# Splitting whole weight tiles of four k-tiles at once, with two raw buffers and three buffers each for hi and lo

## The chip, the cores and the metric

The kernel runs on one core of a Trainium2 chip. The metric is the device time of one launch in microseconds (us), less is better. The engines are called as in the profile: PE (TensorE matmuls; PEld is its weight load), DVE (VectorE), ACT (ScalarE), POOL (GpSimd) and SP (SyncE, which here only issues DMAs). Each engine takes its instructions strictly in the order of its own queue.

## What is computed

One inference step of one layer of a hybrid decoder, for a prompt group (256 tokens) and a sample group (8 sequences of 4 tokens). Both groups use the same weights, so the kernel runs 288 tokens through each matrix. Cut to what matters:

```python
p_mem_k, p_mem_v = rmsnorm(mem) @ w_ck, rmsnorm(mem) @ w_cv       # 256 memory rows, 2048 x 2048 each
z, xbc, dt, q, k, v, r, g, gate_a, gate_b = split(rmsnorm(x) @ w_in)   # 2048 x 15408
branch_a = ssd_scan(conv(xbc), dt, ...) @ w_ssd_out               # 2048 x 2048
branch_b = gla_scan(q, k, v, g, ...) @ w_gla_out                  # 2048 x 2048
h = x + (sigmoid(gate_a) * branch_a + sigmoid(gate_b) * branch_b) @ w_mix_out
h = h + cross_attend(rmsnorm(h), mem_k, mem_v, w_cq, w_co)
a, gt = split(causal_conv(rmsnorm(h) @ w_up))                     # 2048 x 11264
y = rmsnorm(h + (silu(gt) * a) @ w_down)                          # 5632 x 2048
```

All inputs and outputs are float32.

## The kernel before

Matrix products run in the format fp32r. To keep float32 accuracy every operand is split in two: `hi`, a cast to fp32r, and `lo`, what is left (the value less `hi`). A product is then three matmuls: hi x hi, hi x lo, lo x hi. The activations are split once and stay in SBUF. The weights, 732 tiles of about 512 KB, are streamed, and split on their way:

- `wload` (L106) takes a buffer of the tag `raw` (RB = 3 of them) and SP issues the load.
- `wsplit` (L98) works on half a tile, 512 columns: ACT casts `raw` to `whi` (L101), DVE subtracts `whi` from `raw` to `wlo` (L103). There are WB = 5 buffers each of `whi` and `wlo`, of half a tile. A `raw` buffer is free for the next load when both its halves are subtracted; a `whi` or `wlo` buffer when PE has done the matmuls that read it.
- `proj_w` (L118) is the loop of nearly all projections: for 256 output columns (two accumulators in PSUM) it goes over the rows in tiles of four k-tiles (128 rows each), splits each tile in two halves, and issues per half twelve matmuls of 288 columns: L133 and L134 with `whi`, L137 with `wlo`. So a `raw` tile feeds 24 matmuls. When the last rows are done, `cons` reads the accumulator on ACT and DVE: a copy, a gate, a convolution.
- `mem_proj` (L294) makes the memory keys and values, in 8 projections of 512 columns. There a `raw` tile is two k-tiles of 512 columns, and each k-tile takes six matmuls of 512 columns (L315, L316, L319). In the first of them (`prep` is set) the memory rows are loaded (`mt`, L279), transposed and split between the weight tiles, and the order of PE, ACT, DVE and SP is the one written.

Outside that first projection a scheduler orders each engine's queue at compile time, from priorities in program order and its own estimate of times. Time runs as follows: the memory projections to about 194 us; the SSD and GLA projections, woven with the two scans that work on what the previous projections gave, to about 1210 us; the last gate and `w_mix_out` to 1415; attention woven with `w_cq` to 1640; the rest of `w_co` to 1715; the FFN to the end. The FFN's up projection works in groups of 256 columns, 16 k-tiles, so four `raw` tiles, alternating between the value half and the gate half; after each group `ffn_conv` (L1515) does the causal convolution of two accumulators (L1521 to L1533), and after the gate half the product and its split follow (L1568, L1569, L174, L175). The down projection goes through each block's rows in groups of at most two `raw` tiles and adds the accumulators to `h` (L1590).

Of the kernel before, what the change touches and what calls it, by code (L numbers as in the profile page):

```python
# [12 lines left out]
ALU = mybir.AluOpType  # L13
# [5 lines left out]
KT = D // P  # L19
# [10 lines left out]
FF = 5632  # L30
FT = FF // P
BLK = 8
RB = 3
WB = 5
STOP = object()
LNEXP = "natural_log_exp_and_others"
N_MAIN = [64, 64, 48, 64, 64, 64, 64, 48]
# [4 lines left out]
def hybrid_step(ctx: ExitStack, tc: tile.TileContext, I: dict, O: list):  # L42
    nc = tc.nc
    (y_p, y_s, o_pconv, o_pssd, o_pgla, o_pffn, o_pmk, o_pmv, o_sconv, o_sssd, o_sgla, o_sffn) = O
    V, S, G = nc.vector, nc.scalar, nc.gpsimd
    MM, TR = nc.tensor.matmul, nc.tensor.transpose
# [12 lines left out]
    def acc_tiles(n):  # L59

        turn[0] += 1
        return [ps.tile([P, 512], F32, tag=f"acc{turn[0] % 2}", bufs=2, name="acc") for _ in range(n)]
# [32 lines left out]
        return vcol[:, o:o + n]  # L95


    def wsplit(raw):  # L98

        hi = wp.tile(list(raw.shape), F32R, tag="whi", bufs=WB, name="whi")  # L100
        S.copy(hi, raw)  # L101
        lo = wp.tile(list(raw.shape), F32R, tag="wlo", bufs=WB, name="wlo")
        V.tensor_tensor(lo, raw, hi, ALU.subtract)  # L103
        return hi, lo

    def wload(src):  # L106
        raw = wp.tile([P, src.shape[1], src.shape[2]], F32, tag="raw", bufs=RB, name="raw")
        nc.sync.dma_start(out=raw, in_=src)
        return raw
# [3 lines left out]
    def flush():  # L113

        while late:
            late.pop(0)()

    def proj_w(load, ncol, X, nk, cons, N=T):  # L118

        nt = (ncol + P - 1) // P  # L120
        accs = acc_tiles(nt)
        for k0 in range(0, nk, 4):
            kn = min(4, nk - k0)
            raw = load(k0, kn)
            for s0 in range(0, kn, 2):
                hi, lo = wsplit(raw[:, s0:s0 + 2, :])
                for j in range(nt):
                    m = min(P, ncol - j * P)
                    a = accs[j][0:m, 0:N]
                    cs = slice(j * P, j * P + m)  # L130
                    for k in range(2):
                        xh, xl = X(k0 + s0 + k)
                        MM(a, hi[:, k, cs], xh, start=(k0 + s0 + k == 0), stop=False)  # L133
                        MM(a, hi[:, k, cs], xl, start=False, stop=False)  # L134
                    for k in range(2):
                        xh, xl = X(k0 + s0 + k)
                        MM(a, lo[:, k, cs], xh, start=False, stop=(k0 + s0 + k == nk - 1))  # L137
                    if k0 + s0 + 2 == nk:
                        cons(j, a)
                if k0 + s0 == min(4, nk - 2):  # L140
                    flush()
                yield

    def proj(w, c0, ncol, X, nk, cons, row0=0):
        def load(k0, kn):
            return wload(w[row0 + k0 * P:row0 + (k0 + kn) * P, c0:c0 + ncol].rearrange("(k p) n -> p k n", p=P))
        return proj_w(load, ncol, X, nk, cons)
# [104 lines left out]
    with pool("p0") as p0:  # L252
        mn_hi = p0.tile([P, KT, SEQ], F32R, name="mn_hi")
        mn_lo = p0.tile([P, KT, SEQ], F32R, name="mn_lo")


        for r in range(4):
            q = slice(r * NS, (r + 1) * NS)
# [18 lines left out]
        def mem_load(k0):  # L277
            cs = slice(k0 * P, (k0 + 2) * P)
            nc.sync.dma_start(out=mt[:, :, cs], in_=I["mem_prompt"][0, :, cs].rearrange("(i p) c -> p i c", p=P))  # L279
# [14 lines left out]
        def mem_proj(w, hd, dst, prep=None, hold=None):  # L294

            def feed():
                for k0 in range(0, KT, 2):
                    if prep is not None:
                        mem_load(k0)
                    raw = wload(w[k0 * P:(k0 + 2) * P, 512 * hd:512 * hd + 512].rearrange("(k p) n -> p k n", p=P))  # L300
                    for k in range(2):
                        if prep is not None:
                            prep(k0 + k)
                        yield wsplit(raw[:, k:k + 1, :])

            accs = acc_tiles(2)
            ws = feed()
            ready = [next(ws) for _ in range(2)] if prep is not None else []
            for kk in range(KT):
                if prep is None:  # L310
                    ready.append(next(ws))
                hi, lo = ready.pop(0)
                for m in range(2):
                    ms_ = slice(m * P, (m + 1) * P)
                    MM(accs[m], mn_hi[:, kk, ms_], hi[:, 0, :], start=(kk == 0), stop=False)  # L315
                    MM(accs[m], mn_lo[:, kk, ms_], hi[:, 0, :], start=False, stop=False)  # L316
                for m in range(2):
                    ms_ = slice(m * P, (m + 1) * P)
                    MM(accs[m], mn_hi[:, kk, ms_], lo[:, 0, :], start=False, stop=(kk == KT - 1))  # L319
                if prep is not None:  # L320
                    ready += [w_ for w_ in (next(ws, None) for _ in range(2 if kk == 0 else 1)) if w_]
                yield

            def rows():
                t = p0.tile([P, 2, 512], F32, tag="mp", bufs=2, name="mp")
                for m in range(2):
                    S.activation(t[:, m, :], accs[m], ACT.Identity, scale=mrs[:, m:m + 1])
                G.dma_start(out=dst[0, :, hd, :].rearrange("(m p) d -> p m d", p=P), in_=t)
            if hold is None:
                rows()  # L330
            else:
                hold.append(rows)
# [12 lines left out]
        with tc.manual_schedule(engines={mybir.EngineType.PE, mybir.EngineType.Activation, mybir.EngineType.DVE,  # L345
                                        mybir.EngineType.SP}):
            wm = mm_tile()
            for _ in range(9):
                MM(wm[:, 0:P], ones, ones, start=True, stop=True)
            run(mem_proj(I["w_ck"], 0, o_pmk, prep_mem, held))  # L350
# [84 lines left out]
        def x_prep():  # L435
# [15 lines left out]
            for q in range(2):  # L451
# [4 lines left out]
                yield  # L456

        weave(chain(mem_proj(I["w_cv"], 0, o_pmv), mem_proj(I["w_ck"], 1, o_pmk)), x_norm(), 2 * KT, 24)
        weave(chain(mem_proj(I["w_cv"], 1, o_pmv), mem_proj(I["w_ck"], 2, o_pmk)), x_prep(), 2 * KT - 2, 18)


# [8 lines left out]
        def dt_load(k0, kn):  # L470
            raw = wp.tile([P, kn, 112], F32, tag="raw", bufs=RB, name="raw")
            for o, c0, n in ((0, O_DT, 32), (32, O_G, 16)):
                nc.sync.dma_start(out=raw[:, :, o:o + n],
                                  in_=I["w_in"][k0 * P:(k0 + kn) * P, c0:c0 + n].rearrange("(k p) n -> p k n", p=P))
            for k in range(kn):
                G.tensor_copy(raw[:, k, 48:112].rearrange("p (r n) -> p r n", n=16),
                              raw[:, k, 32:48].unsqueeze(1).to_broadcast([P, 4, 16]))
            return raw

        def dt_cons(j, a):  # L480
# [4 lines left out]
            V.tensor_tensor(lr3[64:80, :], a[64:80], lr3[64:80, :], ALU.subtract)  # L485

        run(proj_w(dt_load, 112, X, KT, dt_cons))

        def dt_prep():
# [647 lines left out]
    def gate(o, cons_t, j0=0, j1=KT // 2):  # L1137
        for j2 in range(j0, j1):
            def cons(j, a, j2=j2):
                cons_t(2 * j2 + j, a)  # L1140
            yield from proj(I["w_in"], o + 256 * j2, 256, X, KT, cons)
# [50 lines left out]
    def project(n):  # L1192

        kind, i = units[n]
        dst = ma if kind == "s" else mb
        yield from out_proj(I["w_ssd_out"] if kind == "s" else I["w_gla_out"], i, fin[n], dst, branch_a if n == 3 else None)

    def steps(g, n):
        for _ in range(n):
            if next(g, STOP) is STOP:  # L1200
                return
            yield

    run(start(0))
    for n in range(8):
# [5 lines left out]
        parts = [nxt, gate(O_GA, gate_early, 0, GH)] if n == 0 else [steps(nxt, 16), project(n - 1), nxt]  # L1211
# [15 lines left out]
    for q in range(4):  # L1227
        m = pc.tile([P, 4, T], F32, tag="mar", bufs=2, name="mar")
# [44 lines left out]
    for j2 in range(KT // 2):  # L1273
        def cons(j, a, j2=j2):
            added(hx[j2][:, j, :], 2 * j2 + j, a, vec("norm_cross"), hn, acc)
# [357 lines left out]
    a = acc_tiles(1)[0]  # L1633
# [61 lines left out]
```

## Time and profile before

| | |
|---|---|
| time, median of 3 runs | 2574.29 us (2574.22 to 2579.31) |
| the profiled execution | 2576.44 us, span 2574.7 us |
| granted TensorE clock, mean | 0.997 |
| PE busy | 2554.8 us, 99% of the span |
| DVE / ACT / POOL busy | 67% / 54% / 14% |
| DMA | 513.53 MB, mean 199 GB/s |
| casts `whi` (L101), 1464 | 897.2 us busy, 618 ns each |
| subtractions `wlo` (L103), 1464 | 991.5 us busy, 687 ns each |

The trace is of one execution. Busy is the union of an engine's instructions; matmuls are pipelined, so that a row of 290 ns does not mean that the next starts 290 ns later: a busy PE can still be waiting for a moment, and its pace is read from counts per stretch. In a row of the timeline the first number is the start, the second the duration, both in us, and the bracket tells how long the engine was idle before it and what ended that. In a row of the waits the three numbers are total us, times and the longest.

### The profile page before, as it was taken

The numbers are of one execution on the slowest core, as the hardware profiler recorded it, in microseconds if no ns is written. First come the engines' busy times: TensorE is split into PE (matmuls) and PEld (weight loads), VectorE is DVE, ScalarE is ACT, GpSimd is POOL, SyncE is SP. The second block draws the span as 40 slices with busy tenths as digits, with TensorE's granted clock in tenths as the row PEclk, the third lists the DMA queues.
The fourth block names the chain that finished last, engine by engine and source line by source line (L and its number), as shares of the span: only waits on it lengthen the run. The fifth ranks groups of instructions, "written<-read, shape, count | busy, mean of one in ns | idle before, by whom it ended". The sixth has DMA issues, their size and how long they took to land. (4 is left out here: it accounts for less than half of the span.)

```text
span 2574.7 us, 50424 instructions
## 1 busy us (share of the span) xinstructions
PE 2554.8 (99%) x19119; PEld 2458.4 (95%) x19119; DVE 1714.8 (67%) x3623; ACT 1378.2 (54%) x2751; POOL 355.5 (14%) x519
## 2 busy tenths in 40 slices
PE   9999999999999999999999999999999999999998
PEld 7889999999999999999999989999999999999998
DVE  5656767687767666767566555567777677675765
ACT  7656547665463555544455544445545455454545
POOL 3002101110000000010000222202212122130200
PEclk9999999999999999999999999999999999999999
DMA  8766666666558575777666778755555555555553
GB/s 258 221 215 202 183 188 203 187 203 200 176 181 275 182 251 176 235 227 251 186 208 211 253 257 303 223 162 165 166 174 171 168 164 175 169 168 173 170 170 127
DMA packets 435203, 513.53 MB, mean 199 GB/s; under 512 B 23216, under 2 KB 385072, under 8 KB 434896
## 3 DMA queue, kind: packets, MB, share of 16 engines
q1 hardware_dynamic: 407568, 422.34, 53.5%
q0 software_dynamic: 27360, 87.96, 10.3%
q8 instruction: 150, 2.46, 0.4%
q14 instruction: 93, 0.76, 0.1%
q10 hardware_dynamic: 32, 0.01, 0.0%
HBM read 464.74 MB, written 45.48 MB: 198 GB/s over the span
## 5 line engine op out<-in xcount | busy, mean ns | idle before, releaser
L103 DVE TENSOR_TENSOR wlo<-raw,whi 128x512 fp32r<-128x512 f32 x1464 | 991.5, 687 | 676.6 <-ACT whi L101 657.8
L101 ACT CAST whi<-raw 128x512 fp32r<-128x512 f32 x1464 | 897.2, 618 | 1000.0 <-PE acc L134 783.2
L133 PE MATMUL acc<-xn,whi 128*128 128x288 f32 (+1 forms) x1936 | 554.9, 302 | 0.0
L134 PE MATMUL acc<-xn,whi 128*128 128x288 f32 (+1 forms) x1936 | 541.5, 295 | 0.0
L137 PE MATMUL acc<-xn,wlo 128*128 128x288 f32 (+1 forms) x1936 | 412.1, 294 | 3.4 <-DVE wlo L103 3.4
L134 PE MATMUL acc<-hf,whi 128*128 128x288 f32 x1408 | 392.7, 295 | 0.0
L133 PE MATMUL acc<-hf,whi 128*128 128x288 f32 x1408 | 389.4, 292 | 0.0
L133 PEld LDWEIGHTS acc<-xn,whi 128*128 128x128 f32 (+1 forms) x1936 | 364.3, 188 | 9.3 <-issue 7.9
L134 PEld LDWEIGHTS acc<-xn,whi 128*128 128x128 f32 (+1 forms) x1936 | 364.6, 188 | 6.4 <-issue 4.1
L137 PEld LDWEIGHTS acc<-xn,wlo 128*128 128x128 f32 (+1 forms) x1936 | 311.1, 188 | 4.1 <-DVE wlo L103 4.1
L137 PE MATMUL acc<-hf,wlo 128*128 128x288 f32 x1408 | 296.2, 291 | 0.0
L134 PEld LDWEIGHTS acc<-hf,whi 128*128 128x128 f32 x1408 | 264.5, 188 | 0.1
L133 PEld LDWEIGHTS acc<-hf,whi 128*128 128x128 f32 x1408 | 264.1, 188 | 0.1
L137 PEld LDWEIGHTS acc<-hf,wlo 128*128 128x128 f32 x1408 | 225.9, 188 | 0.0
L1520 POOL COPY fsp<-fst 128x16 f32<-128x16 f32 x88 | 127.6, 1452 | 640.3 <-ACT fca L1526 286.5
L134 PE MATMUL acc<-pr,whi 128*128 128x288 f32 x704 | 196.5, 295 | 0.0
L133 PE MATMUL acc<-pr,whi 128*128 128x288 f32 x704 | 195.6, 294 | 0.0
L137 PE MATMUL acc<-pr,wlo 128*128 128x288 f32 x704 | 147.8, 291 | 0.0
L133 PE MATMUL acc<-un,whi 128*128 128x288 f32 x512 | 146.1, 301 | 0.0
L134 PE MATMUL acc<-un,whi 128*128 128x288 f32 x512 | 143.1, 295 | 0.5 <-DVE un L171 0.5
L134 PEld LDWEIGHTS acc<-pr,whi 128*128 128x128 f32 x704 | 132.3, 188 | 0.0
L133 PEld LDWEIGHTS acc<-pr,whi 128*128 128x128 f32 x704 | 132.1, 188 | 0.0
(515 smaller groups left out, 4243.1 us busy)
## 6 DMA issues: line engine op xcount, KB each, us to landing
raw<-in_w_in_dram SPq DMA_DIRECT2D x240, 512.0 KB
raw<-in_w_up_dram SPq DMA_DIRECT2D x176, 512.0 KB
raw<-in_w_down_dram SPq DMA_DIRECT2D x88, 512.0 KB
raw<-in_w_ck_dram SPq DMA_DIRECT2D x32, 512.0 KB
raw<-in_w_cv_dram SPq DMA_DIRECT2D x32, 512.0 KB
raw<-in_w_ssd_out_dram SPq DMA_DIRECT2D x32, 512.0 KB
sin<-in_state_gla_dram POOLq DMA_DIRECT2D x32, 512.0 KB, 6.2
out_dram<-sin SPq DMA_DIRECT2D x32, 512.0 KB
```

The source lines that it names most:

```text
L101: S.copy(hi, raw)
L103: V.tensor_tensor(lo, raw, hi, ALU.subtract)
L133: MM(a, hi[:, k, cs], xh, start=(k0 + s0 + k == 0), stop=False)
L134: MM(a, hi[:, k, cs], xl, start=False, stop=False)
L137: MM(a, lo[:, k, cs], xh, start=False, stop=(k0 + s0 + k == nk - 1))
L1520: G.tensor_copy(sp[:, :, 0:2], st.rearrange("p (b k) -> p b k", k=2))
```

## The change

`wsplit` becomes a generator over parts of a tile. `proj_w` splits the whole tile of four k-tiles with one cast and one subtraction of 1,024 columns, and so do the memory projections after the first, for their tiles of two k-tiles of 512 columns; the first memory projection still works in pieces of 512 columns, now inside one whole `whi` and `wlo` tile. `whi` and `wlo` have three buffers each of 1,024 columns instead of five of 512; `raw` has two buffers instead of three. The matmuls and their order in the program are the same.

```diff
-RB = 3
-WB = 5
+RB = 2
+WB = 3
...
-    def wsplit(raw):
+    def wsplit(raw, parts=1):
 
         hi = wp.tile(list(raw.shape), F32R, tag="whi", bufs=WB, name="whi")
-        S.copy(hi, raw)
         lo = wp.tile(list(raw.shape), F32R, tag="wlo", bufs=WB, name="wlo")
-        V.tensor_tensor(lo, raw, hi, ALU.subtract)
-        return hi, lo
+        n = raw.shape[1] // parts
+        for q in range(parts):
+            c = slice(q * n, (q + 1) * n)
+            S.copy(hi[:, c], raw[:, c])
+            V.tensor_tensor(lo[:, c], raw[:, c], hi[:, c], ALU.subtract)
+            yield hi, lo
...
             kn = min(4, nk - k0)
-            raw = load(k0, kn)
+            (hi, lo), = wsplit(load(k0, kn))
             for s0 in range(0, kn, 2):
-                hi, lo = wsplit(raw[:, s0:s0 + 2, :])
                 for j in range(nt):
...
-                        MM(a, hi[:, k, cs], xh, start=(k0 + s0 + k == 0), stop=False)
-                        MM(a, hi[:, k, cs], xl, start=False, stop=False)
+                        MM(a, hi[:, s0 + k, cs], xh, start=(k0 + s0 + k == 0), stop=False)
+                        MM(a, hi[:, s0 + k, cs], xl, start=False, stop=False)
...
                     raw = wload(w[k0 * P:(k0 + 2) * P, 512 * hd:512 * hd + 512].rearrange("(k p) n -> p k n", p=P))
+                    split = wsplit(raw, 1 if prep is None else 2)
                     for k in range(2):
                         if prep is not None:
                             prep(k0 + k)
-                        yield wsplit(raw[:, k:k + 1, :])
+                        if prep is not None or k == 0:
+                            hi, lo = next(split)
+                        yield hi[:, k, :], lo[:, k, :]
```

More of the change, by code (lines that the diff above doesn't have):

```diff
@@ L132, in proj_w @@
                         xh, xl = X(k0 + s0 + k)
-                        MM(a, hi[:, k, cs], xh, start=(k0 + s0 + k == 0), stop=False)
-                        MM(a, hi[:, k, cs], xl, start=False, stop=False)
+                        MM(a, hi[:, s0 + k, cs], xh, start=(k0 + s0 + k == 0), stop=False)
+                        MM(a, hi[:, s0 + k, cs], xl, start=False, stop=False)
                     for k in range(2):
                         xh, xl = X(k0 + s0 + k)
-                        MM(a, lo[:, k, cs], xh, start=False, stop=(k0 + s0 + k == nk - 1))
+                        MM(a, lo[:, s0 + k, cs], xh, start=False, stop=(k0 + s0 + k == nk - 1))
                     if k0 + s0 + 2 == nk:
@@ L314, in mem_proj @@
                     ms_ = slice(m * P, (m + 1) * P)
-                    MM(accs[m], mn_hi[:, kk, ms_], hi[:, 0, :], start=(kk == 0), stop=False)
-                    MM(accs[m], mn_lo[:, kk, ms_], hi[:, 0, :], start=False, stop=False)
+                    MM(accs[m], mn_hi[:, kk, ms_], hi, start=(kk == 0), stop=False)
+                    MM(accs[m], mn_lo[:, kk, ms_], hi, start=False, stop=False)
                 for m in range(2):
                     ms_ = slice(m * P, (m + 1) * P)
-                    MM(accs[m], mn_hi[:, kk, ms_], lo[:, 0, :], start=False, stop=(kk == KT - 1))
+                    MM(accs[m], mn_hi[:, kk, ms_], lo, start=False, stop=(kk == KT - 1))
                 if prep is not None:
```

## The prediction

> **What bounds the kernel now.** I read the page's busy times first, then the table of waits with SyncE's own, then a table of stretches, and last the timeline around single weight tiles.
>
> ```profile
> PE 2554.8 (99%) x19119; PEld 2458.4 (95%) x19119; DVE 1714.8 (67%) x3623; ACT 1378.2 (54%) x2751; POOL 355.5 (14%) x519
> ACT whi L101 <- PE acc L134: 783.2, 883, 3.1
> ACT whi L101 <- DMA raw<-in_w_in_dram: 55.7, 25, 5.6
> SPq L108 <- DVE wlo L103: 1493.1, 531, 13.6
> L137 PE MATMUL acc<-xn,wlo 128*128 128x288 f32 x1920 | 408.7, 294 | 3.4 <-DVE wlo L103 3.4
> ```
>
> PE is never free: 2554.8 of 2574.7 us. The casts wait for PE (783.2 us, 883 times, for a `whi` slot that PE has finished with), so the split runs ahead of PE and is held back by it. Only 25 casts waited for a load of `w_in`, and PE's own wait for a `wlo` of that kind is 3.4 us in all. The loads on SP wait for the subtraction that frees a `raw` slot: a load goes out when its slot is free, and the number of slots sets how early that is. Shorter work on ACT and DVE therefore buys next to nothing; the question is whether the loads still come in time.
>
> The time of one weight tile on PE, from the table of stretches (columns: stretch, its length, busy us and count for PE, PEld, DVE, ACT, POOL, granted clock, DMA share, GB/s):
>
> ```profile
> 150.00:200.00 50.00, 50.00 (x223) 41.12 (x222) 26.86 (x50) 25.45 (x43) 1.45 (x2) 1.00 0.70 219
> 500.00:550.00 50.00, 47.98 (x362) 46.57 (x362) 40.20 (x85) 32.82 (x71) 7.02 (x14) 1.00 0.63 186
> 700.00:750.00 50.00, 47.97 (x357) 45.70 (x356) 33.91 (x85) 31.54 (x56) 0.75 (x2) 0.97 0.51 142
> 2150.00:2200.00 50.00, 50.00 (x387) 49.99 (x387) 31.79 (x63) 22.81 (x44) 7.28 (x10) 1.00 0.57 178
> 194.00:1210.00 1016.00, 1011.46 (x7676) 971.67 (x7675) 699.14 (x1442) 562.40 (x1091) 102.94 (x202) 1.00 0.67 206
> 1210.00:1415.00 205.00, 205.00 (x1559) 205.00 (x1558) 125.48 (x226) 101.62 (x186) 9.99 (x17) 1.00 0.67 208
> ```
>
> In the FFN a `raw` tile feeds 24 matmuls: 24 x 50/387 = 3.10 us. In the memory projections it feeds 12 wider ones: 12 x 50/223 = 2.69 us. With two `raw` slots a slot must come round once in two tiles: 6.20 us in the FFN, 5.38 us in the memory projections. With three slots it had 9.3 and 8.1 us.
>
> **What a slot's round costs.** From SP's issue to the cast that waited for that load, and on to the subtraction:
>
> ```profile
> 1961.53 0.37 SPq L108 DMA_DIRECT2D raw<-in_w_up_dram  x1
> 1965.15 0.62 ACT L101 CAST whi<-raw 128x512 fp32r<-128x512 f32 x1 [1.10 <-DMA raw<-in_w_up_dram]
> 1965.80 0.69 DVE L103 TENSOR_TENSOR wlo<-raw,whi 128x512 fp32r<-128x512 f32 x1 [1.03 <-ACT whi L101]
> L103 DVE TENSOR_TENSOR wlo<-raw,whi 128x512 fp32r<-128x512 f32 x1456 | 988.4, 689 | 671.5 <-ACT whi L101 653.1 <-PE acc L316 5.6 <-PE mm L1061 3.9
> L101 ACT CAST whi<-raw 128x512 fp32r<-128x512 f32 x1456 | 894.2, 619 | 994.8 <-PE acc L134 782.8 <-DMA raw<-in_w_in_dram 55.7 <-DVE wlo L103 21.7
> L103 DVE TENSOR_TENSOR wlo<-raw,whi 128x224 fp32r<-128x224 f32 x8 | 3.1, 394 | 5.1 <-ACT whi L101 4.7 <-PE mm L454 0.4
> L101 ACT CAST whi<-raw 128x224 fp32r<-128x224 f32 x8 | 2.9, 380 | 5.2 <-PE acc L316 3.8 <-POOL raw L476 1.0 <-PE acc L134 0.4
> ```
>
> The load took 3.62 us from issue to use. A 1,024-column instruction stands nowhere in this trace. Twice the 512 row bounds it from above (1.24 and 1.38 us); the line through the rows of 224 and 512 columns gives 619 + 512 x 239/288 = 1.04 us for the cast and 689 + 512 x 295/288 = 1.21 us for the subtraction, and I take these, since one instruction pays its fixed part once. Between cast and subtraction lie 0.03 us, between the freed slot and the next issue 0.07 us (the subtraction that starts at 2135.94 and lasts 0.68, and the issue at 2136.69, in the FFN's rows below). The round is 3.62 + 1.04 + 0.03 + 1.21 + 0.07 = 5.97 us. Before, it was 3.62 + half a period 1.55 + 0.62 + 0.03 + 0.69 + 0.07 = 6.58 us, with 9.3 us to do it in. The spare falls from 2.7 us in every three tiles to 0.23 us in every two in the FFN, and in the memory projections it is gone.
>
> The Trainium skill, page "DMA: Bandwidth & Descriptors", section "Anatomy of one DMA", puts one transfer (on the GpSimd path) at about 2.0 us plus bytes over 436 GB/s; for 512 KB that is 3.2 us, an estimate from that page. By it the round would be 5.55 us and the FFN would keep 0.65 us spare; the row of 3.62 us decides.
>
> **The change part by part.** The instruction savings, 732 tiles x (2 x 0.689 - 1.21) = 123 us of DVE and x (2 x 0.619 - 1.04) = 145 us of ACT, lie beside PE and count as nothing; if that cover were gone they would count only where PE waits for the split, which is the next item. The slots for `whi` and `wlo` go from five halves to three whole tiles: PE can have 2 periods less 2.28 us = 3.92 us of lead on a subtraction. That lead is used up once and costs nothing. The indices in the matmuls move no work. What is left is the second `raw` slot, by stage.
>
> *First projection.* It keeps 512-column pieces.
>
> ```profile
> 3.37 0.98 SPq L108 DMA_DIRECT2D raw<-in_w_ck_dram  x1
> 9.99 0.37 SPq L108 DMA_DIRECT2D raw<-in_w_ck_dram  x1
> 13.70 0.62 ACT L101 CAST whi<-raw 128x512 fp32r<-128x512 f32 x1
> ```
>
> The third load goes out at about 9.99 instead of 3.37, and the `mt` load behind it on SP too; 9.99 + 3.62 = 13.6 still meets the cast at 13.70, but each later load is then a tile later. I take 4 us (1 to 6).
>
> *The seven other memory projections*, 56 tiles.
>
> ```profile
> 146.34 0.37 SPq L108 DMA_DIRECT2D raw<-in_w_cv_dram  x1
> 150.09 1.14 ACT L101 CAST whi<-raw 128x512 fp32r<-128x512 f32 x2 [1.46 <-DMA raw<-in_w_cv_dram]
> 149.47 0.37 SPq L108 DMA_DIRECT2D raw<-in_w_ck_dram  x1
> 154.54 0.62 ACT L101 CAST whi<-raw 128x512 fp32r<-128x512 f32 x1 [0.89 <-DMA raw<-in_w_ck_dram]
> ```
>
> Here loads take 3.75 us (146.34 to 150.09) to 5.07 us (149.47 to 154.54), the latter with two others in flight. At most one other can be in flight after the change, so I take 4.1, nearer the first row: a round of 4.1 + 2.35 = 6.45 us against 5.38 us, half the difference a tile: 0.53 x 56 = 30 us. Ends: 3.62 gives 16 us, 5.07 gives 57 us.
>
> *The woven SSD and GLA stage*, 194 to 1210 us, 271 tiles by their casts: a tile lasts 1016/271 = 3.75 us on average, so two last 7.5 us and the round fits unless DVE or ACT is late. The 25 casts that waited for `w_in` with three slots (55.7 us, 2.2 us each) mark the places where it is late, nearly all in this stage; there a load goes out a tile (3.1 us) later than before, and the lead of 3.92 us takes most. The rows of 500 and 700 show that PE has already run out of lead twice. I take 30 us, 1.2 for each of the 25 (10 to 70).
>
> *Gates, output projections, attention*, 1210 to 1715 us: 24 x 205/1559 = 3.16 us a tile outside attention, 0.35 us spare in two; 8 us (0 to 25).
>
> *FFN.* Each group of four tiles ends with a burst of convolution work, and the next tile's cast and subtraction stand in the same queues:
>
> ```profile
> 2130.50 0.42 DVE L1521 TENSOR_TENSOR fu<-acc,rstd 128x256 f32<-128x256 f32 x1
> 2130.80 0.62 ACT L101 CAST whi<-raw 128x512 fp32r<-128x512 f32 x1 [0.94 <-PE acc L134]
> 2131.32 0.60 ACT L1525 ACTIVATE gv<-fu,fcol 128x256 f32<-128x256 f32 x1
> 2134.60 0.68 DVE L103 TENSOR_TENSOR wlo<-raw,whi 128x512 fp32r<-128x512 f32 x1
> 2135.94 1.28 DVE L103 TENSOR_TENSOR wlo<-raw,whi 128x512 fp32r<-128x512 f32 x2
> 2136.69 0.37 SPq L108 DMA_DIRECT2D raw<-in_w_up_dram  x1
> 2143.32 0.62 ACT L101 CAST whi<-raw 128x512 fp32r<-128x512 f32 x1 [0.94 <-PE acc L134]
> 2146.76 2.60 DVE L103 TENSOR_TENSOR wlo<-raw,whi 128x512 fp32r<-128x512 f32 x4
> ```
>
> The cast at 2130.80 is first on ACT, but DVE reaches its subtraction at 2134.60, after the burst. A whole subtraction there ends at 2135.81, 5.01 us after the cast instead of 2.28: 2.73 us late. In the value half it is 2146.76 + 1.21 - 2143.32 = 4.65: 2.37 us late. The slot that meets the burst makes two rounds in four tiles: 2 x 5.97 + 2.73 = 14.67 or 2 x 5.97 + 2.37 = 14.31 us, against 4 x 3.10 = 12.40. That is 2.27 and 1.91 us a group, 92 us over 44 groups (176 tiles). A late load also blocks ACT: L1525 stands behind the cast, and with it the burst on DVE, so waiting does not shorten the delay. The lower end is 0, if the queues are ordered so that the burst goes first (11.94 is under 12.40). The queue order of the rows speaks for the upper end; I take three quarters, 70 us. The down projection (88 tiles) has two evictions in two tiles, about 0.45 us of delay on a round: (6.42 - 6.20)/2 x 88 = 10 us at most; I take 5. FFN: 75 us (0 to 102).
>
> **Sum.** 4 + 30 + 30 + 8 + 75 = 147 us. The profiled execution took 2576.44 us (span 2574.7), 2.15 above the median of 2574.29. 2576.44 + 147 = 2723, and against the median 2721 us. All low ends give 27 us, all high ends 260 us.
>
> **Rivals.** (1) *Only the memory projections and a few places lose.* If the queue order leaves the burst ahead of the cast, or a load in a quieter queue comes under 3.5 us, the FFN's 0.23 us suffices: 4 + 25 + 15 + 5 + 8 = 57 us, 2631. For it: the spare is above 0. The page's 3.2 us a load would lead here. Against: the queue order in the rows. Chance 25%.
>
> (2) *Stalls long enough to lower the clock.*
>
> ```profile
> 728.18 0.29 PE L134 MATMUL acc<-xn,whi 128*128 128x288 f32 x1
> 730.50 0.53 PE L137 MATMUL acc<-xn,wlo 128*128 128x288 f32 x2 [2.03 <-DVE wlo L103]
> 730.00:734.00 4.00, 3.50 (x17) 3.50 (x18) 4.00 (x8) 1.54 (x3) 0.00 (x0) 0.67 0.43 117
> 734.00:738.00 4.00, 4.00 (x30) 4.00 (x29) 1.44 (x4) 1.24 (x3) 0.00 (x0) 0.91 0.91 277
> ```
>
> After one wait of 2.03 us the granted clock was 0.67 and 0.91 for 4 us each: 4 x 0.33 + 4 x 0.09 = 1.7 us lost. If every one of the 44 FFN groups stalls that long in one piece and loses 1.7 us, 75 us come on top: 2796. Against: a PE that waits for loads anyway loses little by a slow clock. Chance 20%. The Trainium skill, "TensorE: Matmul & The Clock Gate", Part 1, has the half rate follow an idle window of about 3.4 us; by it, stalls of 2.3 us would cost no clock, and the row after 2.03 us speaks against that.
>
> (3) *Faster.* DVE's shorter queue takes away the waits for `wlo`: 3.4 us, the 1.7 us of clock behind one of them, and some 2 us in the first projection: 7 us, 2567. It decides only if the round is under 5.38 us in the memory projections, so a load under 3.0 us; no row shows one. Chance 4%.
>
> (4) *No change*, within 5 us: every stage hides the round. Chance 4%.
>
> **How the numbers follow.** The main case has 47% and gives 2721. The range, 2610 to 2820, takes in nearly all of rival 1 and half of rival 2; outside lie rivals 3 and 4 and the tails, some 20%. 0.2% of the time (5 us) is what a measurement of this kernel can tell from none. Faster 0.04, same 0.04, slower 0.92.
>
> **What would show it.** Right: casts of 1.04 and subtractions of 1.21 us; in the waits, `whi` released mainly by the DMA of `raw` instead of by PE; PE idle before L137, L133 and L315 for `wlo` and `whi`; about 2.8 us or more for a memory tile and gaps of about 2 us every four tiles in the FFN's up projection. Wrong: casts that still wait for PE throughout the FFN, which is rival 1; a granted clock under 1 all over the FFN, which is rival 2.

## The result, and the profile after

The changed kernel takes 2665.4 us (median of 4, 2663.92 to 2668.05), the kernel before 2576.6 us in the same runs (4): a ratio of 1.0346, 95% interval 1.0332 to 1.0359, so 89 us slower. The forecast was 2721 us, range 2610 to 2820. Sign and range hold. The sum does not hold in one large term: the FFN (the up and down projections at the end) was to lose 75 us and lost 14.

The page of the changed kernel, first part (busy us, share of the span, instructions):

```profile
PE 2598.2 (97%) x19119; PEld 2472.9 (93%) x19119; DVE 1636.9 (61%) x2899; ACT 1252.2 (47%) x2027; POOL 288.9 (11%) x519
```

DVE does 78 us less than before and ACT 126 us less, and the kernel is slower all the same: the saving lay in time that PE was busy anyway. The new instructions, from the groups by shape (busy us, mean ns | idle before, and what ended it):

```profile
L106 DVE TENSOR_TENSOR wlo<-raw,whi 128x1024 fp32r<-128x1024 f32 x720 | 880.7, 1224 | 794.7 <-ACT whi L105 777.7 <-PE acc L139 6.4 <-PE acc L136 4.0
L105 ACT CAST whi<-raw 128x1024 fp32r<-128x1024 f32 x720 | 755.1, 1049 | 1028.0 <-DMA raw<-in_w_in_dram 285.8 <-PE acc L136 245.2 <-DMA raw<-in_w_up_dram 148.3
```

1224 and 1049 ns stand where 1.21 and 1.04 us were forecast. What holds the casts back has changed, in the table of waits (us, times, longest):

```profile
ACT whi L105 <- DMA raw<-in_w_in_dram: 285.8, 132, 5.9
ACT whi L105 <- PE acc L136: 245.2, 146, 8.4
ACT whi L105 <- DMA raw<-in_w_up_dram: 148.3, 94, 5.2
ACT whi L105 <- DMA raw<-in_w_mix_out_dram: 48.0, 23, 7.9
ACT whi L105 <- DMA raw<-in_w_ck_dram: 43.1, 25, 3.5
```

Casts that waited for PE 783.2 us now do so for 245.2 us; waiting for a load of `w_in` went from 55.7 to 285.8 us. The split is no longer ahead of PE; more of its waiting is now for loads than for PE. How that reaches PE depends on the stage (table of stretches, columns as before):

```profile
34.00:196.00 162.00, 149.81 (x659) 112.60 (x658) 79.77 (x117) 82.92 (x136) 7.55 (x22) 0.99 0.64 197
1510.00:1515.00 5.00, 2.77 (x21) 2.53 (x20) 0.00 (x0) 0.00 (x0) 0.00 (x0) 1.00 1.03 394
1515.00:1520.00 5.00, 3.30 (x14) 3.04 (x15) 2.23 (x2) 4.78 (x5) 0.00 (x0) 0.69 0.38 120
2150.00:2250.00 100.00, 100.00 (x748) 99.98 (x747) 72.65 (x162) 50.14 (x96) 12.93 (x20) 1.00 0.52 161
2250.00:2350.00 100.00, 100.00 (x772) 100.00 (x771) 61.94 (x110) 42.09 (x64) 7.80 (x13) 1.00 0.54 169
```

In the memory projections PE is busy for 149.81 of 162 us, and in attention it stands for almost half of a stretch of 5 us. In the FFN it is busy throughout, with 772 or 748 matmuls in 100 us (24 x 100/772 = 3.11 us a tile, 24 x 100/748 = 3.21), hardly fewer than the 387 in 50 us of before.

To see what each stage lost, I took the start of every weight tile's first matmul in the trace after and subtracted the same tile's start in the trace before. The growth of that difference through each stage is its loss:

| stage (us in the trace of before) | forecast | after |
|---|---|---|
| first projection, to 34 | 4 | 2.0 |
| seven other memory projections, to 194 | 30 | 25.8 |
| woven SSD and GLA, to 1210 | 30 | 30.2 |
| gates and `w_mix_out`, attention, rest of `w_co`, to 1715 | 8 | 20.2 (8.9 + 10.1 + 1.2) |
| FFN, to 2560 | 75 | 13.7 |
| sum | 147 | 91.9 |

The profiled execution took 2668.05 us against 2576.44, 91.6 us more, so the sum closes. Where a stage begins is a choice of tile: the first tile behind 34 us instead of the last one before it moves 1.3 us from the second row to the first. Below, "stage loss" of a kernel is made in this way, always against the same trace of before.

### The profile page after: what moved, and what is told of

Same layout as the page of the kernel before. It is cut to its first block, busy times and chain, and to the rows that moved or that the text cites. A ratio compares the mean times of both kernels' runs of the same rounds, so it can differ in the third digit from the quotient of the medians.

```text
span 2666.3 us, 47771 instructions
## 1 busy us (share of the span) xinstructions
PE 2598.2 (97%) x19119; PEld 2472.9 (93%) x19119; DVE 1636.9 (61%) x2899; ACT 1252.2 (47%) x2027; POOL 288.9 (11%) x519
## 4 chain that ended last, share of the span: by engine, by line
PE 61%; DMA 21%; DVE 9%; ACT 7%; issue 2%; POOL 0%; ACTq 0%; SPq 0%; DVEq 0%; POOLq 0%
PE acc L136 18%; PE acc L135 18%; PE acc L139 17%; DMA raw<-in_w_in_dram 8%; DVE wlo L106 6%; ACT whi L105 5%; DMA raw<-in_w_mix_out_dram 2%; DMA raw<-in_w_cv_dram 2%; DMA raw<-in_w_ck_dram 2%; DMA raw<-in_w_cq_dram 2%; DMA raw<-in_w_up_dram 1%; DMA raw<-in_w_co_dram 1%; PE mm L1328 1%; DMA raw<-in_w_ssd_out_dram 1%; PE la L1377 1%
## 5 line engine op out<-in xcount | busy, mean ns | idle before, releaser
L106 DVE TENSOR_TENSOR wlo<-raw,whi 128x1024 fp32r<-128x1024 f32 (+2 forms) x740 | 894.3, 1209 | 812.2 <-ACT whi L105 795.1
L105 ACT CAST whi<-raw 128x1024 fp32r<-128x1024 f32 (+2 forms) x740 | 767.1, 1037 | 1043.7 <-DMA raw<-in_w_in_dram 285.8
L1525 POOL COPY fsp<-fst 128x16 f32<-128x16 f32 x88 | 55.9, 638 | 718.9 <-DVE av L1537 369.5
```

The source lines that it names most:

```text
L105: S.copy(hi[:, c], raw[:, c])
L106: V.tensor_tensor(lo[:, c], raw[:, c], hi[:, c], ALU.subtract)
L1525: G.tensor_copy(sp[:, :, 0:2], st.rearrange("p (b k) -> p b k", k=2))
```

## The experiments

**Are two raw slots alone enough to make it slow?** The kernel before, with nothing changed but the slots:

```diff
-RB = 3
+RB = 2
```

> The kernel before with two raw buffers; pieces of 512 columns and five buffers each of hi and lo as before. Theory A: most of the loss is here already, 2630 to 2720 us (a slot's round is 3.6 us of load plus 1.9 to 2.9 us for the two halves, by whether PE paces the second half). Rival B: it is the coarse pieces, so this one stays under 2600 us.

Measured: 2716.37 us (2712.92 to 2732.93), ratio 1.0532 [1.05, 1.0564]. The slot alone makes it slow, and slower than the whole change does. Stage losses here are 18.5 (memory), 47.7 (woven), 31.9 (gates to `w_co`) and 41.2 us (FFN), against 25.8, 30.2, 20.2 and 13.7 of the changed kernel: the change's other half, whole tiles in three buffers, costs time in the memory projections and saves it in the other stages. Its waits:

```profile
ACT whi L101 <- DMA raw<-in_w_in_dram: 292.7, 148, 6.9
ACT whi L101 <- DMA raw<-in_w_up_dram: 186.9, 118, 5.0
ACT whi L101 <- PE acc L134: 180.6, 171, 4.8
```

The picture is that of the changed kernel, with twice as many casts and subtractions.

**Does the third slot take it all back?** The changed kernel with RB = 3. For the room three buffers of other tags go, so the kernel before with the same three cuts ran beside it as the control:

```diff
-RB = 2
+RB = 3
...
-        return pa.tile(shape, F32, tag="c4", bufs=6, name=name)
+        return pa.tile(shape, F32, tag="c4", bufs=5, name=name)
...
-            sq = pb.tile([P, T], F32, tag="sq", bufs=2, name="sq")
+            sq = pb.tile([P, T], F32, tag="sq", bufs=1, name="sq")
...
-        return px.tile([P, 2, 256], F32R, tag="q2", bufs=6, name=name)
+        return px.tile([P, 2, 256], F32R, tag="q2", bufs=5, name=name)
```

> The changed kernel with three raw buffers instead of two, and three whole buffers each of hi and lo. To make room, three other tags have one buffer less (c4 6 to 5, q2 6 to 5, sq of the FFN pool 2 to 1). Theory A (the whole loss is the second raw buffer: a slot's round of about 6 us against two tile periods): the time of before or of the control with the same three tags cut, 2570 to 2585 us; casts wait for PE again. Rival B (the coarser pieces cost: 1,024-column instructions block ACT and DVE, and whole tiles are released later): a good part of the 89 us stays, 2610 us or more.

> The kernel before with the same three tags cut by one buffer (c4, q2, sq of the FFN pool), nothing else. Both theories: within 10 us of before, 2570 to 2587 us. It prices what the room for the third raw buffer costs by itself.

Measured: 2618.48 us, ratio 1.0141 [1.0124, 1.0158], and the control 2614.17 us, ratio 1.0121 [1.0106, 1.0137]. The control missed its expectation: cutting the three buffers costs 32 us by itself, 28.0 of them in the woven stage. Against the control the whole tile with three slots costs 4 us by the medians, and the two intervals overlap. The two profiled executions lie 11 us apart, and by stages that is 1.9 us worse in the memory projections, 1.7 better in the woven stage, 4.1 worse in the gates and 6.4 worse in the FFN. In its waits

```profile
ACT whi L105 <- PE acc L136: 686.2, 400, 6.5
ACT whi L105 <- DMA raw<-in_w_in_dram: 18.7, 9, 6.0
```

the casts wait for PE again. So nearly all of the 89 us hangs on the number of `raw` slots, if the cuts cost as much beside whole tiles as they do beside halves.

**The third slot without the cuts.** Three `raw`, three `whi`, but two `wlo`, which is the room that the change has:

```diff
-RB = 2
+RB = 3
...
-        lo = wp.tile(list(raw.shape), F32R, tag="wlo", bufs=WB, name="wlo")
+        lo = wp.tile(list(raw.shape), F32R, tag="wlo", bufs=WB - 1, name="wlo")
```

> The changed kernel with three raw buffers, three whole buffers of hi and two of lo, which is the memory of before to the byte; no other tag is cut. Theory A: no waits for loads, so faster than the changed kernel: 2580 to 2625 us; what is left comes from the subtraction, which has to wait until PE has finished with the tile two back. Rival B (coarse pieces): 2640 us or more.

Measured: 2615.02 us, ratio 1.0135 [1.0112, 1.0157], as expected. The memory projections lose 1.8 us and the FFN 2.3, but the woven stage still loses 23.1 us and attention 10.3, and the subtraction has a new wait:

```profile
DVE wlo L106 <- PE acc L139: 300.8, 194, 2.9
ACT whi L105 <- DMA raw<-in_w_in_dram: 100.3, 43, 6.5
```

A subtraction that waits for a `wlo` slot also keeps its `raw` slot, and 43 casts still wait for `w_in`. So the two `wlo` buffers seem to hold back `raw` as well; that is read from the waits.

**The same memory dealt otherwise.** Four `raw` and two each of `whi` and `wlo`:

```diff
-RB = 2
-WB = 3
+RB = 4
+WB = 2
```

> The changed kernel with the same memory dealt out otherwise: four raw buffers, two whole buffers each of hi and lo. Theory A (a raw slot's round sets the time): four slots give four periods, 12.4 us, to a round of about 6 us, so no cast waits for a load for long, and what is lost is lost by the short lead of the split: a subtraction may start when PE has finished the tile two back and ends 2.3 us later, one period (3.1 us) before PE needs it, so every delay over 0.8 us reaches PE. 2600 to 2650 us, faster than the changed kernel. Rival B (coarse pieces are the cost): slower than the changed kernel, since the coarse release now bites with two slots, over 2675 us.

Measured: 2591.87 us (10 runs), ratio 1.0038 [1.0023, 1.0053]: better than I expected, but still 0.4% slower than the kernel before, and the interval leaves out 1. No cast waits for `w_in` any more; casts wait for PE, 677.7 us:

```profile
ACT whi L105 <- PE acc L136: 677.7, 386, 5.4
DVE wlo L106 <- ACT whi L105: 619.1, 480, 2.9
```

What is left is 10.2 us in the woven stage and 9.0 in the FFN; where it comes from was not tried.

**And with the halves of before?** Four `raw` and four halves each of `whi` and `wlo`, in the kernel before, could have been the better version:

```diff
-RB = 3
-WB = 5
+RB = 4
+WB = 4
```

> The kernel before with RB 3 to 4 and WB 5 to 4: the same 32 KB a partition, still one cast and one subtraction for each 512 columns. Theory A (what counts is the number of raw slots times the period of a tile against the round from issue to subtraction; split slots above about one tile are spare): the 25 waits for w_in (55.7 us of ACT's time, of which PE felt a few us) become fewer than 10 and nothing else moves, since PE was already busy for 99% of the span; 2570 to 2582 us, so within 0.4% of the kernel before. Rival (the split lead matters too: with four halves PE has only two tiles' worth of split work in hand, and a burst in DVE's queue reaches PE): PE's wait for wlo in the FFN and the woven stage grows from under 5 us to 20 or more, and the time is 2590 us or more.

Measured: 2578.22 us (11 runs) against 2575.58, ratio 1.0007 [0.9994, 1.002], no difference. Of the casts that waited for `w_in` (25, 55.7 us) none is left:

```profile
ACT whi L101 <- PE acc L134: 902.9, 1012, 3.1
```

By stages it is 0.3 us faster in the woven stage, where nearly all of these waits were, 3.2 faster in the memory projections and 5.2 slower in the FFN. So the 25 waits cost the kernel before nothing that can be measured, although a small gain could hide behind a small loss from having four halves of each kind instead of five.

**Is it the round of a slot?** By the theory, two slots that go round in R us give a tile every R/2 us, if that is longer than PE needs. Doing the subtraction twice in the seven memory projections adds one subtraction (1.22 us) to R and leaves PE's work as it is:

```diff
-    def wsplit(raw, parts=1):
+    def wsplit(raw, parts=1, times=1):
...
-            V.tensor_tensor(lo[:, c], raw[:, c], hi[:, c], ALU.subtract)
+            for _ in range(times):
+                V.tensor_tensor(lo[:, c], raw[:, c], hi[:, c], ALU.subtract)
...
-                    split = wsplit(raw, 1 if prep is None else 2)
+                    split = wsplit(raw, 1 if prep is None else 2, 2 if prep is None else 1)
```

> The changed kernel; in the seven memory projections after the first, the subtraction of every tile is done twice (the same result written again), so a raw slot's round there is longer by one subtraction, 1.15 to 1.2 us, and nothing else changes. Theory A (with two slots a tile lasts half a round wherever that is longer than PE's work): a tile of these 56 goes from 3.28 us to about 3.85, the stage takes 56 x 0.58 = 32 us more, the whole 28 to 36 us more than the changed kernel. Rival L (the loads themselves, or the bandwidth, pace the stage): DVE is 49% busy there, so the second subtraction fits beside the loads and costs under 8 us.

Measured: 2697.93 us, ratio 1.0438 [1.0421, 1.0456] to the before of its own runs; 32.5 us over the changed kernel by the two medians, 24 us by the two ratios (the kernel before ran 7 us slower beside this one). The forecast of theory A was 28 to 36. The traces have it by stage: the memory projections lose 61.6 us instead of 25.8, and no other stage moves by more than 3.3 us. A tile there took 3.89 us instead of 3.28, which is half a subtraction more. DVE, the third of the five busy times in a row, is not full meanwhile:

```profile
34.00:230.00 196.00, 159.13 (x674) 116.28 (x673) 132.96 (x163) 84.03 (x137) 8.49 (x22) 0.98 0.54 166
100.00:150.00 50.00, 40.73 (x167) 29.44 (x165) 34.69 (x37) 19.55 (x27) 1.45 (x2) 0.97 0.55 167
```

34.69 of 50 us: nobody is busy all the time, and the round sets the pace. I also took each load's round, from its issue to the end of its subtraction, out of the traces. Half of the mean round against the mean time between tiles:

| kernel, stage | half a round | between tiles | between tiles before |
|---|---|---|---|
| after, memory | 3.25 | 3.28 | 2.78 |
| after, FFN | 3.19 | 3.20 | 3.15 |
| two slots with halves, memory | 3.13 | 3.18 | 2.78 |
| two slots with halves, FFN | 3.29 | 3.30 | 3.15 |

The two agree within 2% everywhere. On its own that would only say that both slots are always in use; that adding 1.22 us to the round lengthened the tile by half of it shows which way the cause runs.

**Pieces instead of whole tiles.** The changed kernel with two casts and two subtractions of 512 columns a tile, the slots as in the change:

```diff
-            (hi, lo), = wsplit(load(k0, kn))
+            pieces = wsplit(load(k0, kn), kn // 2)
             for s0 in range(0, kn, 2):
+                hi, lo = next(pieces)
...
-                    split = wsplit(raw, 1 if prep is None else 2)
+                    split = wsplit(raw, 2)
...
```

> The changed kernel, but each whole tile is cast and subtracted in two pieces of 512 columns, so that DVE works on the first piece while ACT casts the second: from cast to the end of the subtraction 0.62 + 0.53 + 0.03 + 0.69 = 1.9 us instead of 2.3. Buffers as changed: two raw, three whole hi and lo. Theory A: the round is 0.4 us shorter, so 10 to 50 us of the loss come back, 2615 to 2655 us. Rival B: the 512-column pieces bring the time back to under 2600 us. If the number of instructions mattered, it would be slower than the changed kernel, over 2670 us.

Measured: 2712.96 us, ratio 1.0498 [1.0473, 1.0522]: a miss. The memory projections are faster than with whole tiles (18.3 against 25.8 us), since the first subtraction runs beside the second cast: from the first cast to the last subtraction's end it is 2.0 us on average instead of 2.3. But the woven stage loses 46.0 us and the FFN 45.1. The time is near that of two slots with five halves (2716.37 us), so the pieces make the difference to the changed kernel and not the number of split buffers. The number of instructions, which the expectation names for a time over 2670 us, does not explain it: the memory projections gain with the same pieces, the control above with 1,464 casts is no slower than the 740 of the changed kernel with three slots, and the next experiment loses more with the instructions of the changed kernel. In the FFN the pieces' subtractions stand behind the burst of the convolution (timeline of DVE, that kernel, some rows left out; the casts came at 2267.00):

```profile
2267.50 0.48 DVE L1538 SCALAR_TENSOR_TENSOR av<-fu,fcol,av 128x254 f32<-128x254 f32 x1
2268.50 0.25 DVE L1537 SCALAR_TENSOR_TENSOR av<-fsp,fcol,av 128x32 f32<-128x32 f32 x1
2268.66 0.69 DVE L106 TENSOR_TENSOR wlo<-raw,whi 128x512 fp32r<-128x512 f32 x1
2269.42 1.89 DVE L106 TENSOR_TENSOR wlo<-raw,whi 128x512 fp32r<-128x512 f32 x3
```

On DVE that is the order of the kernel before. What the pieces cost in the woven stage was not traced further. The changed kernel has another order at such a place, which the forecast had not seen. ACT, then DVE, some rows left out:

```profile
2215.61 0.60 ACT L1530 ACTIVATE gv<-fu,fcol 128x256 f32<-128x256 f32 x1 [1.63 <-DVE fu L1526]
2216.31 1.05 ACT L105 CAST whi<-raw 128x1024 fp32r<-128x1024 f32 x1
2217.26 0.60 ACT L1530 ACTIVATE gv<-fu,fcol 128x256 f32<-128x256 f32 x1
```

```profile
2217.37 0.18 DVE L1527 TENSOR_TENSOR fsp<-acc,rstd 128x32 f32<-128x32 f32 x1
2217.47 1.21 DVE L106 TENSOR_TENSOR wlo<-raw,whi 128x1024 fp32r<-128x1024 f32 x1
2218.61 0.44 DVE L1574 TENSOR_TENSOR gv<-gv,av 128x288 f32<-128x288 f32 x1
```

The cast stands behind the burst's first activation (L1525 of before, now L1530), and the subtraction stands in the middle of the burst, ahead of the gated product. From the cast to the subtraction's end it is 2.37 us here, against 5.01 us in the forecast.

**Two places of the queue order of before, held fast.** The changed kernel, and for each group of the FFN's up projection two added edges of order, without a semaphore: the burst's first activation behind the cast of the tile that meets it, and that tile's subtraction behind the last multiply-add or the first gated product:

```diff
+    def pin(first, second):
+        tc.add_manual_dep(second.ins, first.ins.name, mybir.DependencyInfo(
+            mybir.DependencyClass.NoSync, mybir.DependencyReason.DATA), reason="order")
...
+        seen[0] += 1
+        late_act, early_dve = pins.pop(seen[0], (None, None))
...
+            if late_act is not None:
+                pin(cast, late_act)
+                pin(early_dve, sub)
...
```

> The changed kernel; in the FFN alone the order of two queues is pinned as in the trace of before: on ACT the cast of the tile that meets the burst stands ahead of the first activation of the convolution (L1543 here), on DVE its subtraction stands behind the last multiply-add of the value half, or behind the first gated product of the gate half. Nothing else is changed. Theory Q (the FFN lost 14 us and not 75 because the scheduler moved these two instructions): cast to subtraction of that tile rises from 2.4 to 4 us or more, the FFN loses 40 to 90 us against before, and the whole takes 30 to 80 us more than the changed kernel, 2695 to 2750 us. Rival S (late casts would have caught up anyway, since DVE is idle between bursts): within 15 us of the changed kernel, 2665 to 2690 us.

Measured: 2769.76 us (2764.58 to 2780.2), ratio 1.0748 [1.0711, 1.0786], 104 us over the changed kernel by the medians and above the 2695 to 2750 that I expected. The FFN loses 114.8 us instead of 13.7, the other stages within 2.1 us of the changed kernel's. Of the 114.8, 90.7 fall to the up projection and 24.1 to the down projection, and 17.8 of these to the third tile of its six blocks: it meets the last burst of the up projection, and its places were held as well. One burst, ACT and then DVE, some rows left out (the lines have moved: L115 and L116 are the cast and the subtraction, L1543 the burst's first activation):

```profile
2273.11 1.05 ACT L115 CAST whi<-raw 128x1024 fp32r<-128x1024 f32 x1 [2.46 <-DMA raw<-in_w_up_dram]
2274.07 1.09 ACT L1543 ACTIVATE gv<-fu,fcol 128x256 f32<-128x256 f32 x2
2282.31 1.05 ACT L115 CAST whi<-raw 128x1024 fp32r<-128x1024 f32 x1 [4.17 <-DMA raw<-in_w_up_dram]
```

```profile
2276.84 0.83 DVE L1589 TENSOR_TENSOR gv<-gv,av 128x288 f32<-128x288 f32 x2 [0.38 <-ACT gv L1588]
2277.59 1.22 DVE L116 TENSOR_TENSOR wlo<-raw,whi 128x1024 fp32r<-128x1024 f32 x1
2278.72 0.82 DVE L190 TENSOR_TENSOR pr<-gv,pr 128x288 fp32r<-128x288 f32 x2
```

The subtraction ends 5.70 us after its cast, and the cast for the slot that it frees waits 4.17 us for its load. In the stretches (2250 to 2350 us) PE is now idle in the FFN too:

```profile
2250.00:2350.00 100.00, 94.15 (x688) 92.92 (x687) 57.79 (x106) 39.19 (x61) 5.80 (x16) 0.97 0.50 154
```

688 matmuls where the changed kernel has 772, with the same instructions and buffers. The two edges are what was added; around them the scheduler moved more: by the traces other instructions of the burst on ACT and DVE, and on PE pairs of matmuls at some 40 places and 17 transposes of the caches. So the 104 us are the price of the two held places with all that followed from them.

## Why the prediction was right or wrong, step by step

**The two slots as the bound: right.** The round of a slot was worked out as load, cast, subtraction, next issue, and the change as a race of that round against two tiles. Two slots alone are slow, three take nearly all of it back (if the three small buffers cost the same beside both kernels), and lengthening the round by 1.22 us lengthened a tile by 0.61 us.

**The savings on ACT and DVE at nothing: right.** 78 and 126 us of busy time went (forecast 123 and 145), and no stage became faster than before.

**First projection, 4 us: 2.0. Memory projections, 30 us: 25.8.** Casts that waited for a load came 4.27 us after its issue on average (4.1 taken), and the round was 6.50 us (6.45). The tile of before was 2.78 us over the whole stage, not the 2.69 of the 50 us that I had read; with it the same sum gives 25 us.

**Woven stage, 30 us: 30.2, by luck: the working does not stand.** I took 1.2 us for each of the 25 casts that had waited for `w_in`. Four slots in the kernel before removed those waits and brought no time, and the change has 132 of them. That the stage hangs on the slots is shown by three slots against their control (26.3 and 28.0 us), with the same condition as above; how its 30 us are spread over the 132 waits stays open.

**Gates, output projections, attention, 8 us: 20.2, too small.** The term was carried by the FFN's load of 3.62 us. In the gates the casts that waited came 4.26 us after the issue, so that the round is 4.26 + 2.35 = 6.61 us against 6.32 us: half the difference for 65 tiles (205/3.16) is 9 us, and 8.9 was measured. In attention the 13 casts that waited came 6.88 us after it on average, seven of them 3.5 to 5.5 and six 8.6 to 10.7. One such place, in the timeline of ACT and in the DMA view of 1495 to 1515 us (queues: packets, MB, share of the 16 DMA engines; issues: KB each, median us to landing):

```profile
1515.17 1.04 ACT L105 CAST whi<-raw 128x1024 fp32r<-128x1024 f32 x1 [8.29 <-DMA raw<-in_w_cq_dram]
```

```profile
q0 software_dynamic: 800, 2.92, 41.7%
q1 hardware_dynamic: 2486, 2.48, 37.7%
kc<-in_cache_mem_k_dram POOLq DMA_DIRECT2D x5, 512.0 KB, 7.4
```

The loads that POOL issues (q0), among them those of the cache, take as much of the DMA engines there as SP's queue with the weight loads (q1) does; the stretch 1510 to 1515 above has a DMA share of 1.03 and 394 GB/s. That they lengthen the weight load is read from this, and was not tried.

**FFN, 75 us: 13.7. This is the step that failed.** It was the up projection: 70 us forecast, 7.3 lost, while the down projection was to lose 5 and lost 6.4. The working took the queue order of before for the order of the change: "The queue order of the rows speaks for the upper end." The queues are ordered at compile time, from estimates of time, and an instruction of 1,024 columns was put at another place than two of 512: the experiment with pieces differs in that size and has DVE's old order. The subtraction of the tile that meets the burst ended 2.4 and 2.5 us after its cast on average (the two kinds of group) against 2.3 us at quiet places and against the 5.01 and 4.65 forecast. The number of slots is not what moved it: with three slots it is 2.4 and 2.5 us with whole tiles, and 5.1 and 4.7 with halves (the control). With the delay gone the round nearly fits: loads of 3.77 us where the cast waited for them and a mean round of 6.38 us against 6.20, a tile of 3.20 us against 3.15 before. Those 0.05 us x 264 tiles are the 13 us. With the two places held fast the up projection lost 90.7 us, where the forecast's upper end was 92, and the four rounds that a slot makes in eight tiles took 29.6 us, where the forecast has 14.67 + 14.31 = 28.98: the price was right, and the condition was not met. The order that came out is near to rival 1's condition (a part of the burst stands ahead of the tile, not all of it), and its 8 us for the FFN is near to the 14; its 2631 is too low because it gave the other stages 49 us, and they lost 78. That the total still fell into the range is owed to the range, which reached down to rival 1, and not to the main case.

The Trainium skill, "DMA: Bandwidth & Descriptors", section "Anatomy of one DMA", led to an estimate of 3.2 us a load; its figures are for the GpSimd path, and these loads are issued by SP. From the issue to the cast that waited the mean here was 3.77 us in the FFN and 4.27 in the memory projections, so the trace does not agree; the FFN was saved by the queue order and not by a quick load.

**Rival 2, the clock: not seen.** In the FFN, PE had no stalls to speak of, and the granted clock was 1.00 in both stretches shown. With the two places held fast it was 0.97 over 1800 to 2720 us, at most 28 of these 920 us; what part of that kernel's loss this is was not separated.

**What would show it.** Casts of 1.04 and subtractions of 1.21 us, `whi` released by the DMA of `raw`, and over 2.8 us for a memory tile were there. The gaps of 2 us every four tiles in the FFN were not there, and this was the sign of the failed step. Casts that still wait for PE in the FFN, the sign of rival 1, were there in part: 84 of them, beside 114 that waited for a load.

## What to carry to other kernels

A buffer that is filled by a DMA goes round in load + wait + use, measured from the trace; slots x time of a tile must exceed that with the worst place of the queues in it, and when memory is short a raw slot may be worth more than a slot for what is made of it. Here four raw and two split buffers of each kind came within 0.4% of the kernel before, and two and three in the same room lost 3.5%. When the size of an instruction changes and a scheduler orders the queues, the order of before isn't that of after: price both orders, and read the new one first when the result comes.

## What had not been expected

- The place of two instructions a group in two queues, with the same instructions and buffers and with what the scheduler moved around them, is worth 104 us (2769.76 against 2665.4).
- With two slots, merging two instructions lengthens the round in one stage (the memory projections lose 25.8 us with whole tiles, 18.3 with pieces) and shortens it in others, by where the queues put it (FFN 13.7 against 45.1).
- Cutting one buffer each of three small tags cost the kernel before 32 us; a control without the change in question was needed to see it.
- In attention a 512 KB weight load on SP's queue took 6.88 us on average from issue to use where the cast waited for it, against 3.77 in the FFN; POOL's loads were in flight there, and that they are the cause was not tried.
